# Attention's division by the row sums, moved from the probabilities to o, and two moves beside it

## The chip, the cores and the metric

One NeuronCore of one Trainium2 chip runs the whole block. The time is device microseconds of one execution; the kernel before takes 2336.07 us (median of 3 runs, 2334.95 to 2337.75). The engines are called TensorE (PE), VectorE (DVE), ScalarE (ACT) and GpSimd (POOL); SP's queue issues most of the DMAs, GpSimd's queue the rest.

## The reference, cut to what matters

A layer of 1024 tokens of width 1024: a SwiGLU feed-forward, a mixer, a second SwiGLU feed-forward, each followed by a residual and a layer norm, all in float32. The mixer holds 8 attention heads of 64 columns beside a gated linear recurrence, and an output projection over both. The attention, in blocks of 128 queries:

```python
s = einsum('bhqd,bhkd->bhqk', qh[:, :, q0:q1], kh[:, :, :q1]) * scale
s = s + cum[:, :, q0:q1, None] - cum[:, :, None, :q1]
s = where(mask, s, -1e30)
p = softmax(s, axis=-1)
outs.append(einsum('bhqk,bhkd->bqhd', p, vh[:, :, :q1]))
```

The softmax divides every row of exponentials by its sum. The same o comes out when the values are summed with the exponentials themselves and each row of o is divided by its sum afterwards.

## The kernel before, in words

The stages run one after the other: the first feed-forward (gate/up by Strassen's seven products of blocks, then down), the mixer's input projections with the recurrence, attention with the output projection, the second feed-forward. Every float32 matrix product is done as three matmuls of the type fp32r, of parts called hi and lo: hi is the rounded copy that ScalarE writes, lo is what is left, which VectorE gets by a subtraction.

Attention (`attention`) goes through 64 units, a head h and a block i of 128 queries. Heads 0 to 5 run one after the other, each from i = 7 (1024 keys) down to i = 0 (128 keys); the units of heads 6 and 7 are interleaved. Three functions make a unit:

- `probs(h, i)`: TensorE makes the scores in a bank pair `s` (lines 991 and 992), of which there are two. GpSimd masks the diagonal block of the row `cum`, which is the head's cumulated forget gate, loaded once a head (line 995). VectorE adds cum to the scores, writes p and finds the row's minimum in one instruction (line 997). ScalarE takes the exponential and its sum (line 998). VectorE inverts the sum (line 999) and GpSimd multiplies p by it (line 1000).
- `to_pT(h, i, p)`, three units later: TensorE transposes p in squares of 128 (line 1011) into banks `a`, of which there are four; ScalarE and VectorE write the hi and lo parts `pt` (lines 1015 and 1016).
- `values(h, qt)`, one unit later still and for every second i: TensorE multiplies v by pt for 256 queries (line 1027). ScalarE and VectorE put o together, 64 rows a head, so that heads 2c and 2c + 1 fill one tile of 128 rows whose columns are the queries (lines 1030 and 1031). After the odd head, ScalarE and VectorE write the hi and lo parts `mix` of these 128 rows (lines 1034 and 1035). For heads 1, 3 and 5 GpSimd's queue stores them to memory (line 1038), and SP's queue loads them again shortly before the output projection; those of head 7 are used where they are.

Between the units stand tiles of the output projection (`down_tile`): 16 of them, over the recurrence's part, fill units of heads 0 to 4; the 16 over the attention's part come behind the values of head 7, each followed, when a row block is done, by the layer norm on VectorE and a store of the rows by GpSimd's queue (line 1163). After them the blocks for the second gate/up are transposed and split (line 248).

`load(h)` brings a head's q, k, cum and v; two heads have room. The tiles `raw`, two in number, take weights on their way in: the four halves of the output projection's, and then the first two loads, each in two halves, of the second gate/up (`first_raws`, line 264, called at the end of the kernel function).

The order of the instructions of every engine and queue is fixed when the program is built: a scheduler walks through what the code records, picks by priority and readiness after its own estimates of durations, and gives room in the tile pools and the waits between engines. An engine then works through its own list in that order, each instruction waiting for what it needs. `tc.issue_after(x)` adds one rule: what is recorded in its block stands behind x on x's engine. The tiles `fgz` (128 x 8 x 8), `wf` (128 x 8 x 8) and `gate_raw` (128 x 2 x 128) belong to the mixer's input stage and are not used by attention before the change.

Of the kernel before, what the change touches and what calls it, by code (L numbers as in the profile page):

```python
# [12 lines left out]
AF = mybir.ActivationFunctionType  # L13
ALU = mybir.AluOpType
# [3 lines left out]
P = 128  # L18
# [7 lines left out]
HEADS = 8  # L26
# [22 lines left out]
def f32(ap):  # L49
    return ap.bitcast(F32)  # L50


class Block:
# [903 lines left out]
    def attention(self, w_out, mixp, ln, normed):  # L957

        nc, v = self.nc, self.nc.vector
# [5 lines left out]
        with self.pool("att_p", 3) as pp, self.pool("att_t", 1) as tp, self.pool("att_pt", 6) as ptp, self.pool("att_qk", 2, side="right") as qkp:  # L965

            def load(h):
                vt = qkp.tile([P, NT, P], F32R, tag="v", name=self.nm("v"))
                cum = qkp.tile([P, T], F32, tag="cum", name=self.nm("cum"))
                q, kh, kl = (qkp.tile([P, T], F32R, tag=t, name=self.nm(t)) for t in ("q", "kh", "kl"))  # L970
                mine = slice(64 * (h % 2), 64 * (h % 2) + 64)
                for j in range(2):
                    rows = slice(64 * j, 64 * j + 64)
                    nc.sync.dma_start(f32(q[rows]), self.q_d[h // 2, j, mine, :])
                    nc.sync.dma_start(f32(kh[rows]), self.k_d[h // 2, 0, mine, :])
                    nc.sync.dma_start(f32(kl[rows]), self.k_d[h // 2, 1, mine, :])
                row = self.cum_d[h:h + 1, :]
                nc.sync.dma_start(cum, bass.AP(tensor=row.tensor, offset=row.offset, ap=[[0, P], [1, T]]))
                nc.sync.dma_start(f32(vt), self.v_d[h].rearrange("(j p) d -> p j d", p=P))
                return q, kh, kl, vt, cum  # L980

            def probs(h, i):

                q, kh, kl, _, cum = heads[h]
                n = (i + 1) * P
                ts = slice(i * P, n)
                s = self.s_tile()
                for bank in range((n + H - 1) // H):
                    c1 = min(max(n - bank * H, 256), H)
                    cols = slice(bank * H, bank * H + c1)  # L990
                    mm(s[:, bank, 0:c1], q[:, ts], kh[:, cols], start=True, stop=False)
                    scores = mm(s[:, bank, 0:c1], q[:, ts], kl[:, cols], start=False, stop=True)
                sf = s.rearrange("p b c -> p (b c)")
                p = pp.tile([P, T], F32, tag="p", name=self.nm("p"))
                nc.gpsimd.affine_select(cum[:, ts], cum[:, ts], pattern=[[-1, P]], compare_op=ALU.is_ge, fill=1e30, base=0, channel_multiplier=1)
                m = self.small.tile([P, 4], F32, tag="m", name=self.nm("m"))
                v.tensor_tensor_reduce(p[:, 0:n], sf[:, 0:n], cum[:, 0:n], 1.0, 3e38, ALU.add, ALU.min, m[:, 1:2])
                nc.scalar.activation(p[:, 0:n], p[:, 0:n], AF.Exp, bias=m[:, 1:2], scale=-1.0, accum_out=m[:, 2:3])
                v.reciprocal(m[:, 3:4], m[:, 2:3])
                nc.gpsimd.tensor_scalar(p[:, 0:n], p[:, 0:n], m[:, 3:4], 1.0, op0=ALU.mult, op1=ALU.mult)  # L1000
                return p, scores

            def to_pT(h, i, p):
                if i % 2:
                    pts[h, i // 2] = [tuple(ptp.tile([P, 4, 256], F32R, tag="pt", name=self.nm("pt")) for _ in range(2))
                                      for _ in range((i + 4) // 4)]
                for g in range((i + 4) // 4):
                    js = range(4 * g, min(4 * g + 4, i + 1))
                    pa = self.a_tile()
                    for j in js:  # L1010
                        nc.tensor.transpose(pa[:, (j % 4) * P:(j % 4 + 1) * P], p[:, j * P:(j + 1) * P], self.ident)  # L1011
                    w = len(js)
                    pav = pa.rearrange("p (j t) -> p j t", j=4)[:, 0:w, :]
                    hi, lo = (x[:, 0:w, (i % 2) * P:(i % 2 + 1) * P] for x in pts[h, i // 2][g])
                    nc.scalar.copy(hi, pav)
                    v.tensor_tensor(lo, pav, f32(hi), ALU.subtract)

            def values(h, qt):
                vt = heads[h][3]
                b = h % 2  # L1020
                rows, rest = slice(64 * b, 64 * b + 64), slice(64 - 64 * b, P - 64 * b)
                pv = self.a_tile()
                last = 2 * qt + 1
                for j in range(last + 1):
                    ps = slice(P, 256) if j == last else slice(0, 256)
                    for l in range(2):
                        mm(pv[:, ps], vt[:, j, :], pts[h, qt][j // 4][l][:, j % 4, ps], start=j == 0 and l == 0, stop=j == last and l == 1)  # L1027
                cols = slice(qt * 256, (qt + 1) * 256)
                t = outs[h // 2]
                nc.scalar.copy(t[rows, cols], pv[rest, 0:256])  # L1030
                v.tensor_tensor(t[rows, cols], t[rows, cols], pv[rows, 0:256], ALU.add)
                if b:
                    hi, lo = (x[:, cols] for x in mixes[h // 2])
                    nc.scalar.copy(hi, t[:, cols])
                    v.tensor_tensor(lo, t[:, cols], f32(hi), ALU.subtract)
                    if qt == 0 and h < HEADS - 1:
                        for l in range(2):
                            nc.gpsimd.dma_start(mix_d[h // 2][l], f32(mixes[h // 2][l]))
# [8 lines left out]
            fill = [(i, d) for i in range(NT) for d in range(2)]  # L1047
            AHEAD = 3
            heads[0] = load(0)

            def out_tile():
# [6 lines left out]
            for n in range(len(units) + AHEAD + 1):  # L1058
                if n < len(units):
                    h, i = units[n]  # L1060
                    if i == 5 and h < 6 or (h, i) == (6, 6):
                        heads[h + 1] = load(h + 1)
                    if i == NT - 1:
                        if h % 2 == 0:
                            outs[h // 2] = tp.tile([P, T], F32, tag="o", name=self.nm("o"))
                        else:
                            mixes[h // 2] = tuple(mixp.tile([P, T], F32R, tag="h", name=self.nm("mix")) for _ in range(2))
                    ps[n], scores = probs(h, i)
                if 0 <= n - AHEAD < len(units):
                    to_pT(*units[n - AHEAD], ps.pop(n - AHEAD))  # L1070
                if 0 <= n - AHEAD - 1 < len(units):
                    h, i = units[n - AHEAD - 1]
                    if i % 2 == 0:
                        values(h, i // 2)
                        if h == HEADS - 1:
                            tiles += [(i + 1, 0), (i + 1, 1), (i, 0), (i, 1)]
                if fill and (n < 2 or n % 8 in (2, 3, 4)):
                    i, d = fill.pop(0)
# [16 lines left out]
def kernel(  # L1095
# [7 lines left out]
    nc = tc.nc  # L1103
    blk = Block(ctx, tc)
# [5 lines left out]
    with blk.pool("xl", side="right") as xl, blk.pool("x1") as x1, blk.pool("gu_t", 4) as tp, blk.pool("x22") as x22, \  # L1110
# [13 lines left out]
        raws, load = blk.first_raws(ffn1_w_gate[0], ffn1_w_up[0])  # L1124
# [53 lines left out]
    with blk.pool("xl") as xl, blk.pool("gu_t", 4) as tp, blk.banks() as bank:  # L1178
        blk.open_blocks(xl, REST)
        raws, load = blk.first_raws(ffn2_w_gate[0], ffn2_w_up[0])  # L1180
        load(0)
        load(1)
        finish = blk.gate_up(ffn2_w_gate[0], ffn2_w_up[0], h_d[1], rows, bank, tp, wsp, raws, js=(3, 2, 1, 0))
    right.close()
    with blk.psum(), blk.pool("dn_ws", 10) as blk.wsp, blk.pool("dn_v", side="right") as vp, blk.pool("dn_w", side="right") as wp:
# [40 lines left out]
```

## Time and profile before

| | |
|---|---|
| median of 3 runs | 2336.07 us |
| the profiled execution's own time | 2336.28 us |
| its span, first to last instruction | 2334.6 us |
| TensorE busy | 2305.4 us, 99% |
| VectorE busy | 1632.3 us, 70% |
| ScalarE busy | 1011.3 us, 43% |
| GpSimd busy | 223.0 us, 10% |

Busy time is the union of an engine's instructions. Matmuls overlap one another in the pipeline and their ends are modelled, so TensorE counts as busy for a moment after it has stopped issuing. A matmul of 512 columns is shown for 0.39 us. The time of a stage is read from the stretch in which it runs: attention lies between about 1176 and 1400 us.

### The profile page before, as it was taken

To read this page: it belongs to the slowest core of one execution; us is meant where nothing else is said; L and a number is where in the kernel's file an instruction comes from. 1 tells how busy PE (TensorE), PEld (TensorE's weight loads), DVE (VectorE), ACT (ScalarE), POOL (GpSimd) and SP (SyncE) were. 2 spreads that over 40 slices of the span, in tenths; PEclk is the share of its full clock that TensorE was granted. 3 is DMA by queue.
4 is the path that set the end of the run, shared out by engine and by line. 5 is a ranking of instruction groups with operands and counts; after the bars stand their busy time and mean duration, and the time that the engine had idled before them with its cause. 6 is when DMAs were issued, how large, how long until landed. Compare 5 with 4: busy or idle time off the path is not lost.

```text
span 2334.6 us, 28297 instructions
## 1 busy us (share of the span) xinstructions
PE 2305.4 (99%) x10721; PEld 1915.5 (82%) x10721; DVE 1632.3 (70%) x2509; ACT 1011.3 (43%) x1587; POOL 223.0 (10%) x364
## 2 busy tenths in 40 slices
PE   9999999999999999999999899999999999999998
PEld 7788888888888888888888787888888888888887
DVE  8766566666567888866667899665656565567886
ACT  6443333434344345454546745433333333344342
POOL 0020000000000000011134510000000000000000
PEclk9999999999999999999999999999999999999999
DMA  4333232323465424132365812332323232564531
GB/s 145 129 94 118 86 118 86 117 86 117 144 244 215 164 109 128 56 110 91 109 190 145 244 55 78 112 110 94 118 86 120 92 125 87 182 246 175 181 144 72
DMA packets 175977, 298.93 MB, mean 128 GB/s; under 512 B 8209, under 2 KB 100689, under 8 KB 175841
## 3 DMA queue, kind: packets, MB, share of 16 engines
q1 hardware_dynamic: 152768, 218.16, 28.5%
q0 software_dynamic: 23072, 78.97, 9.2%
q8 instruction: 84, 1.38, 0.2%
q14 instruction: 53, 0.43, 0.1%
HBM read 214.22 MB, written 82.87 MB: 127 GB/s over the span
## 4 chain that ended last, share of the span: by engine, by line
PE 88%; DVE 5%; issue 3%; DMA 2%; ACT 1%; POOL 1%; SPq 0%; DVEq 0%; POOLq 0%; ACTq 0%
PE x L156 9%; PE x L157 9%; PE x L158 9%; PE b L156 7%; PE b L157 7%; PE b L158 7%; PE s L158 6%; PE s L157 6%; PE s L156 6%; PE a L157 6%; PE a L158 6%; PE a L156 6%; PE a L1027 1%; PE a L1011 1%; DMA raw<-in_ffn_w_gate_dram 1%
## 5 line engine op out<-in xcount | busy, mean ns | idle before, releaser
L283 ACT CAST ws<-t 128x512 fp32r<-128x512 f32 x240 | 149.1, 623 | 394.1 <-PE b L157 266.9
L283 ACT CAST ws<-raw 128x512 fp32r<-128x512 f32 x180 | 112.0, 623 | 258.9 <-PE x L157 256.9
L284 DVE TENSOR_TENSOR ws<-raw,ws 128x512 fp32r<-128x512 f32 x180 | 123.8, 688 | 140.3 <-ACT ws L283 136.8
L284 DVE TENSOR_TENSOR ws<-t,ws 128x512 fp32r<-128x512 f32 x240 | 164.3, 685 | 70.5 <-ACT ws L283 68.6
L156 PE MATMUL b<-As,ws 128*128 128x512 f32 x512 | 199.6, 390 | 0.9 <-ACT As L319 0.5
L157 PE MATMUL a<-ws,ws 128*128 128x512 f32 x512 | 199.7, 390 | 0.2
L156 PE MATMUL a<-ws,ws 128*128 128x512 f32 x512 | 199.3, 390 | 0.4 <-ACT row L523 0.4
L157 PE MATMUL b<-As,ws 128*128 128x512 f32 x512 | 199.6, 390 | 0.0
L156 PE MATMUL x<-As,ws 128*128 128x512 f32 x512 | 199.5, 390 | 0.0
L158 PE MATMUL b<-As,ws 128*128 128x512 f32 x512 | 199.3, 389 | 0.0
L158 PE MATMUL x<-As,ws 128*128 128x512 f32 x512 | 199.2, 389 | 0.0
L158 PE MATMUL a<-ws,ws 128*128 128x512 f32 x512 | 199.2, 389 | 0.0
L157 PE MATMUL x<-As,ws 128*128 128x512 f32 x512 | 199.2, 389 | 0.0
L156 PE MATMUL x<-A,ws 128*128 128x512 f32 x496 | 193.5, 390 | 1.0 <-DVE row L517 0.9
L158 PE MATMUL x<-A,ws 128*128 128x512 f32 x496 | 193.2, 390 | 0.7 <-DVE ws L325 0.7
L157 PE MATMUL x<-A,ws 128*128 128x512 f32 x496 | 193.0, 389 | 0.0
L618 ACT CAST ws<-raw 128x1024 fp32r<-128x1024 f32 x112 | 117.4, 1050 | 158.5 <-PE a L157 87.6
L553 POOL DMA_DIRECT2D h_d<-row x96 | 68.8, 719 | 1148.7 <-DVE row L547 1109.6
L621 DVE TENSOR_TENSOR ws<-raw,ws 128x1024 fp32r<-128x1024 f32 x112 | 136.5, 1220 | 50.2 <-ACT ws L618 49.7
L156 PE MATMUL s<-ws,ws 128*128 128x512 f32 x384 | 149.5, 389 | 0.0
L158 PE MATMUL s<-ws,ws 128*128 128x512 f32 x384 | 149.4, 389 | 0.0
L157 PE MATMUL s<-ws,ws 128*128 128x512 f32 x384 | 149.4, 389 | 0.0
(249 smaller groups left out, 5227.1 us busy)
## 6 DMA issues: line engine op xcount, KB each, us to landing
raw<-h_d SPq DMA_DIRECT2D x56, 1024.0 KB, 5.6
h_d<-row POOLq DMA_DIRECT2D x96, 512.0 KB, 3.7
wd<-in_ffn_w_down_dram SPq DMA_DIRECT2D x32, 1024.0 KB, 7.9
raw<-in_ffn_w_gate_dram SPq DMA_DIRECT2D x30, 1024.0 KB, 5.4
raw<-in_ffn_w_up_dram SPq DMA_DIRECT2D x30, 1024.0 KB, 5.4
h_d<-row POOLq DMA_DIRECT2D x32, 256.0 KB, 2.6
raw<-in_w_in_dram SPq DMA_DIRECT2D x16, 512.0 KB, 5.1
row<-in_x_dram SPq DMA_DIRECT2D x12, 512.0 KB, 8.9
```

The lines of the kernel that those rows point to most:

```text
L156: mm(out, ah, bh, start=first, stop=False, skip_group_check=goes_on)
L157: mm(out, ah, bl, start=False, stop=False, skip_group_check=goes_on)
L158: mm(out, al, bh, start=False, stop=last, skip_group_check=goes_on)
L283: nc.scalar.copy(hi, src)
L284: v.tensor_tensor(lo, src, f32(hi), ALU.subtract)
L553: nc.gpsimd.dma_start(d[:, 2 * n:2 * n + 2], t.rearrange("p (r t) -> p r t", r=2))
L618: cast = nc.scalar.copy(hi, src)
L621: self.mark = v.tensor_tensor(lo, src, f32(hi), ALU.subtract)
L1011: nc.tensor.transpose(pa[:, (j % 4) * P:(j % 4 + 1) * P], p[:, j * P:(j + 1) * P], self.ident)
L1027: mm(pv[:, ps], vt[:, j, :], pts[h, qt][j // 4][l][:, j % 4, ps], start=j == 0 and l == 0, stop=j == last and l == 1)
```

## The change

The reciprocal and the multiplication leave `probs`; p stays as the exponentials. The sums go to `fgz`, one column for each head and block. In `to_pT`, for the odd head of a pair and every even i, VectorE inverts the four sums of two heads and two blocks into `wf` in one instruction, and GpSimd copies them, each 64 times, into `gate_raw`. In `values` of the odd head, TensorE transposes the two halves of `gate_raw` into a bank `a`, which gives the reciprocals in the layout of o, and VectorE multiplies the 128 rows and 256 columns of o by them before the hi and lo parts are made. The lo parts of heads 1, 3 and 5 are made by GpSimd, those of head 7 by VectorE as before. Last, the first four loads of the second gate/up stand behind the load of v of the last head in SP's queue.

```diff
--- before.py
+++ after.py
@@ -976,8 +976,10 @@
                     nc.sync.dma_start(f32(kl[rows]), self.k_d[h // 2, 1, mine, :])
                 row = self.cum_d[h:h + 1, :]
                 nc.sync.dma_start(cum, bass.AP(tensor=row.tensor, offset=row.offset, ap=[[0, P], [1, T]]))
-                nc.sync.dma_start(f32(vt), self.v_d[h].rearrange("(j p) d -> p j d", p=P))
+                self.last_load = nc.sync.dma_start(f32(vt), self.v_d[h].rearrange("(j p) d -> p j d", p=P))
                 return q, kh, kl, vt, cum
+
+            sums, inv = self.fgz, self.wf.rearrange("p h i -> p (h i)").rearrange("p (h i) -> p h i", h=HEADS)
 
             def probs(h, i):
 
@@ -995,9 +997,7 @@
                 nc.gpsimd.affine_select(cum[:, ts], cum[:, ts], pattern=[[-1, P]], compare_op=ALU.is_ge, fill=1e30, base=0, channel_multiplier=1)
                 m = self.small.tile([P, 4], F32, tag="m", name=self.nm("m"))
                 v.tensor_tensor_reduce(p[:, 0:n], sf[:, 0:n], cum[:, 0:n], 1.0, 3e38, ALU.add, ALU.min, m[:, 1:2])
-                nc.scalar.activation(p[:, 0:n], p[:, 0:n], AF.Exp, bias=m[:, 1:2], scale=-1.0, accum_out=m[:, 2:3])
-                v.reciprocal(m[:, 3:4], m[:, 2:3])
-                nc.gpsimd.tensor_scalar(p[:, 0:n], p[:, 0:n], m[:, 3:4], 1.0, op0=ALU.mult, op1=ALU.mult)
+                nc.scalar.activation(p[:, 0:n], p[:, 0:n], AF.Exp, bias=m[:, 1:2], scale=-1.0, accum_out=sums[:, h, i:i + 1])
                 return p, scores
 
             def to_pT(h, i, p):
@@ -1014,6 +1014,11 @@
                     hi, lo = (x[:, 0:w, (i % 2) * P:(i % 2 + 1) * P] for x in pts[h, i // 2][g])
                     nc.scalar.copy(hi, pav)
                     v.tensor_tensor(lo, pav, f32(hi), ALU.subtract)
+                if i % 2 == 0 and h % 2:
+                    r = inv[:, h - 1:h + 1, i:i + 2]
+                    v.reciprocal(r, sums[:, h - 1:h + 1, i:i + 2])
+                    nc.gpsimd.tensor_copy(self.gate_raw.rearrange("p u (b d) -> p u b d", b=2),
+                                          r.rearrange("p b u -> p u b").unsqueeze(3).to_broadcast([P, 2, 2, 64]))
 
             def values(h, qt):
                 vt = heads[h][3]
@@ -1030,9 +1035,13 @@
                 nc.scalar.copy(t[rows, cols], pv[rest, 0:256])
                 v.tensor_tensor(t[rows, cols], t[rows, cols], pv[rows, 0:256], ALU.add)
                 if b:
+                    pr = self.a_tile()
+                    for u in range(2):
+                        nc.tensor.transpose(pr[:, u * P:(u + 1) * P], self.gate_raw[:, u], self.ident)
+                    v.tensor_tensor(t[:, cols], t[:, cols], pr[:, 0:256], ALU.mult)
                     hi, lo = (x[:, cols] for x in mixes[h // 2])
                     nc.scalar.copy(hi, t[:, cols])
-                    v.tensor_tensor(lo, t[:, cols], f32(hi), ALU.subtract)
+                    (nc.gpsimd if h < HEADS - 1 else v).tensor_tensor(lo, t[:, cols], f32(hi), ALU.subtract)
                     if qt == 0 and h < HEADS - 1:
                         for l in range(2):
                             nc.gpsimd.dma_start(mix_d[h // 2][l], f32(mixes[h // 2][l]))
@@ -1178,8 +1187,9 @@
     with blk.pool("xl") as xl, blk.pool("gu_t", 4) as tp, blk.banks() as bank:
         blk.open_blocks(xl, REST)
         raws, load = blk.first_raws(ffn2_w_gate[0], ffn2_w_up[0])
-        load(0)
-        load(1)
+        with tc.issue_after(blk.last_load.ins):
+            load(0)
+            load(1)
         finish = blk.gate_up(ffn2_w_gate[0], ffn2_w_up[0], h_d[1], rows, bank, tp, wsp, raws, js=(3, 2, 1, 0))
     right.close()
     with blk.psum(), blk.pool("dn_ws", 10) as blk.wsp, blk.pool("dn_v", side="right") as vp, blk.pool("dn_w", side="right") as wp:
```

## Rows read from the trace of the kernel before

**Rows 1.** Stretches: length, busy us by engine (instructions), TensorE clock, DMA share, GB/s.
```profile
1206.00:1228.20 22.20, 21.83 (x139) 19.34 (x137) 16.34 (x44) 13.51 (x32) 8.24 (x16) 1.00 0.51 120
1284.00:1340.00 56.00, 47.29 (x309) 39.28 (x309) 47.89 (x122) 44.10 (x101) 28.65 (x49) 1.00 0.90 254
1340.00:1400.00 60.00, 59.32 (x312) 48.65 (x312) 55.92 (x130) 27.64 (x61) 9.79 (x20) 1.00 0.13 53
1400.00:1450.00 50.00, 47.72 (x238) 38.67 (x237) 49.86 (x84) 28.26 (x49) 1.06 (x2) 1.00 0.19 64
1475.00:1500.00 25.00, 25.00 (x112) 20.68 (x112) 17.83 (x27) 8.51 (x15) 2.71 (x4) 1.00 0.30 104
```

**Rows 2.** Waits, 1275 to 1400 us: us in total, times, longest.
```profile
PE s L991 <- DVE m L997: 4.3, 8, 1.5
...
DVE m L999 <- ACT p L998: 2.1, 6, 0.6
...
PE a L1011 <- POOL p L1000: 1.5, 3, 0.5
...
PE a L1011 <- DVE pt L1016: 1.2, 2, 0.9
...
PE a L1027 <- DVE pt L1016: 0.9, 1, 0.9
...
PE a L1011 <- DVE m L999: 0.6, 1, 0.6
...
PE a L156 <- DVE o L1031: 0.3, 1, 0.3
```

**Rows 3.** Groups of VectorE, 1175 to 1400 us: busy us, mean ns, idle before.
```profile
L1031 DVE TENSOR_TENSOR o<-o,a 64x256 f32<-64x256 f32 x32 | 13.3, 415 | 5.3 <-ACT o L1030 4.4
L999 DVE RECIPROCAL m<-m 128x1 f32<-128x1 f32 x64 | 10.1, 158 | 7.2 <-ACT p L998 6.7
...
L1035 DVE TENSOR_TENSOR mix<-o,mix 128x256 fp32r<-128x256 f32 x16 | 6.7, 419 | 0.7 <-ACT mix L1034 0.5
```

**Rows 4.** Groups of GpSimd, whole span, the multiplication at two widths.
```profile
L1000 POOL TENSOR_SCALAR p<-p,m 128x1024 f32<-128x1024 f32 x8 | 9.0, 1123 | 0.0
...
L1000 POOL TENSOR_SCALAR p<-p,m 128x256 f32<-128x256 f32 x8 | 3.8, 480 | 5.5 <-DVE m L999 5.4
```

**Rows 5.** GpSimd in order of time: start us, us, instruction, xcount [idle before, releaser].
```profile
1302.35 3.20 POOL L1000 TENSOR_SCALAR p<-p,m 128x896 f32<-128x896 f32 x2
...
1309.36 0.29 POOL L995 TENSOR_SCALAR_AFFINE_SELECT cum<-cum 128x128 f32<-128x128 f32 x1 [3.56 <-DMA cum<-cum_d]
...
1338.25 1.05 POOL L185 TENSOR_SCALAR gb<-gb 128x1024 f32<-128x1024 f32 x1 [2.20 <-DMA gb<-in_ln_g_dram]
...
1353.43 0.58 POOL L1163 DMA_DIRECT2D x_d<-row  x1 [6.28 <-DVE m L999]
```

**Rows 6.** TensorE in order of time: eight transposes in a row, and one alone.
```profile
1283.07 1.04 PE L1011 MATMUL a<-ident,p 128*128 128x128 f32 x8
...
1299.70 0.27 PE L1011 MATMUL a<-ident,p 128*128 128x128 f32 x1
```

**Rows 7.** SP's DMA queue in order of time: start us, us to issue.
```profile
1298.21 0.53 SPq L978 DMA_DIRECT2D cum<-cum_d  x1
...
1304.17 0.53 SPq L264 DMA_DIRECT2D raw<-in_ffn_w_gate_dram  x1
...
1323.15 0.57 SPq L264 DMA_DIRECT2D raw<-in_ffn_w_up_dram  x1
...
1331.45 0.42 SPq L95 DMA_DIRECT2D gb<-in_ln_g_dram  x1
```

**Rows 8.** Tile raw, 1270 to 1420 us: ns min/median/max, first and last start.
```profile
L319 ACT CAST ws<-raw x4: 604/618/626, 1381.5 to 1398.1; 128x512 fp32r<-128x512 f32 x4
```

**Rows 9.** Groups of VectorE, line 999: 1284 to 1340, then 1340 to 1400 us.
```profile
L999 DVE RECIPROCAL m<-m 128x1 f32<-128x1 f32 x21 | 3.3, 158 | 1.4 <-ACT p L998 1.2
...
L999 DVE RECIPROCAL m<-m 128x1 f32<-128x1 f32 x8 | 1.2, 151 | 0.5 <-ACT p L998 0.3
```


## The prediction

> **What bounds the kernel now.** I cut the span into stretches first. In the feed-forward stages TensorE is busy 25.00 of 25.00 us and issues 112 matmuls of 512 columns in them, one every 0.223 us [rows 1]; a change pays only where TensorE pauses or is given less to do. Attention, from about 1176 to 1400 us, is not one stretch but three. Up to 1284 us each head takes about 22 us and TensorE is busy 21.83 of 22.20 us: its matmuls are the bound. From 1284 to 1340 us (heads 4 to 6 and the start of 7), where few output-projection tiles are left to fill in, it is busy 47.29 of 56.00 us: 8.7 us of visible idling, with VectorE at 47.89 and the DMA engines at 0.90 of their time. From 1340 to 1450 us TensorE (59.32 of 60, 47.72 of 50) and VectorE (55.92 of 60, 49.86 of 50) are both nearly full [rows 1]. The change acts in all three, so each gets its own term.
>
> The waits say what ends the 8.7 us: 4.3 us for the score banks, which VectorE's minimum on line 997 sets free late, and 1.5 + 1.2 + 0.9 + 0.6 = 4.2 us at the transposes (line 1011) and values (line 1027), on GpSimd's multiplication, on VectorE's reciprocal ahead of it, or on the low part that follows [rows 2].
>
> **What is removed.** The 64 reciprocals of line 999 take 10.1 us of VectorE, 0.158 each [rows 3], and make VectorE wait for the exponential: 2.1 us of its waiting between 1275 and 1400 us [rows 2]. The 64 multiplications on GpSimd stand between exponential and transposes in every unit: 0.48 us for 256 columns, 1.12 for 1024 [rows 4], and more when something is in the way: two at 1302.35 took 3.20 us together, and at 1309.36 GpSimd stood 3.56 us behind the load of the next head's cum row, with a multiplication queued behind it [rows 5]. Neither remains between exponential and transposes.
>
> **What is added, by engine.** TensorE: two transposes of 128 columns for each of 4 odd heads x 4 column blocks, 32. Eight of line 1011 took 1.04 us together and one lasts 0.27, so the next starts after (1.04 - 0.27) / 7 = 0.11 us [rows 6]; 32 x 0.11 = 3.5 us, 0.88 per odd head. VectorE: 16 reciprocals of 128x2x2, of which no row exists: between the 0.158 of one column and the 0.42 of 128x256 [rows 3]; I take 0.16, as four elements are nearest to one. And 16 multiplications of 128x256 out of PSUM, bounded by line 1031 (0.415, half the partitions) and line 1035 (0.419, from SBUF) [rows 3]: 0.42 each. In heads 1, 3 and 5 the low part of o (0.419 x 4) leaves VectorE and pays for that. Net for VectorE, per head of 8 reciprocals (1.26 us): even heads -1.26, heads 1, 3, 5 -1.26 + 0.64 = -0.6, head 7 -1.26 + 0.64 + 1.68 = +1.1. GpSimd: 16 copies and 12 subtractions of 256 columns, no rows of either; from below VectorE's 0.42, from above the 1.12 of a 1024-column multiplication [rows 3, 4]. I take 0.5, near the 0.48 of the same width; 14 us in all against 64 multiplications of 0.48 us and more [rows 4], so GpSimd gets lighter. The subtractions have only the store of o's parts behind them. New waits: VectorE's multiplication waits for the two transposes, and queued behind it are o's hi and lo parts and the next unit's line 997, which frees a score bank; the transposes wait for GpSimd's copy and take one of the four banks a, 16 times. The copies are read by TensorE one unit later, over 2 us in heads 1 to 6, and that is their cover; without it, each costs TensorE up to 1.1 us.
>
> The Trainium skill (TensorE: Matmul & The Clock Gate, Part 4: PE-mode transpose) gives some 275 ns for one transpose in a kernel. The trace's duration for one agrees (0.27 us), but the next starts 0.11 us later [rows 6]. By the page's figure as a price the 32 would cost 8.8 us, 5.3 more than I charge.
>
> **What is moved.** The four first loads of the second gate/up (512 KB each). Three go out from 1304.17 us on in SP's queue, ahead of head 7's loads and 6 us behind the issue of head 6's cum row (1298.21), for which GpSimd waits until 1309.36; the fourth comes after head 7's v, at 1323.15 [rows 5, 7]. Now all four stand behind that v. Their first reader is at 1381.5 us [rows 8], so they are not late; what they are moved in front of can be: the last mix tiles and gb, gb at 1331.45. GpSimd already waits 2.20 us for gb [rows 5, 7]. At the stretch's 254 GB/s [rows 1] 1.5 MB are 5.9 us. I take zero to come of it, because the engines are 0.90 full from 1284 to 1340 us and the same bytes have left the queue earlier; if that cover fails, head 7's masks behind gb's sign change are late by up to 5.9 us.
>
> **The sum**, against the profiled run's own time, 2336.28 us (span 2334.6 and 1.7 around it); the median of the runs shown, 2336.07, is 0.2 lower.
> - Up to 1284 us, TensorE-bound: heads 1 and 3 pay 1.76 us of transposes. Against that, TensorE idles 0.37 us of a head [rows 1]; half of the 1.1 us of three heads may go as VectorE is freed of the reciprocals. +1.2 us (+0.7 to +1.8).
> - 1284 to 1340 us: the 4.2 us of waits on the multiplication's chain go, and perhaps half (2.1) of the 4.3 us on line 997, since VectorE loses 3.3 us of reciprocals here [rows 9], gains 0.64 for head 5's, and loses its waits for the exponential. Each pause also lasts longer than the idle time shown, since a transpose counts as busy for 0.27 us and the next could have started after 0.11 [rows 6]; ten pauses less, 1.6 us. Head 5 pays 0.9. That is -7.0. What is late next is VectorE itself (47.9 us of work, then about 45) and the cum loads, so I take -6.0. Ends: -10.5 (8.7 + 1.6 all gone, with little paid) and +0.9 (only the transposes seen).
> - From 1340 us on, both engines full: VectorE has head 7's 2.3 us more, less the eight reciprocals left by then (1.2) [rows 9]; TensorE has 0.9 us more. The chain from values to the output tile grows by the multiplication (0.42) and a semaphore, while nine of the tile's twelve matmuls (2.0 us) cover it; as it already stops TensorE once for 0.3 us on o [rows 2], I charge the three together 1.5 us (0 to +4).
> Sum +1.2 - 6.0 + 1.5 = -3.3: **2333.0 us**.
>
> **Rivals.**
> 1. *The middle stretch closes entirely.* For it: nearly half of its waits are by rows the multiplication's [rows 2], and the three loads leave the queue in which head 6's cum is late. Against it: VectorE and the DMA engines are already near full there [rows 1]. -9.5 there, +1.0 before, +1.0 behind: 2328.8 us.
> 2. *Hidden anyway.* VectorE's order, not the multiplication, sets the pace of heads 4 to 6 (the 4.3 us on line 997, and VectorE busy 86%); the freed waits come back on line 997. Then -2.0 in the middle, +1.8 and +1.5 elsewhere: 2337.6 us.
> 3. *GpSimd's queue in head 7 (slower).* The copies of the reciprocals go into the queue that also stores the layer-normed rows, and such a store waits for VectorE: 6.28 us at 1353.43 [rows 5]. A copy behind one makes TensorE stop in order at the two transposes, and no tile passes them. One output tile (12 x 0.223 = 2.7 us) covers part; each costs 3.6 us. Two of them eat up the gain (2333.0 + 7.2 = 2340.2, slower than before); three give 2343.8 us. Against it: multiplications stood in that queue too, and TensorE waits for one three times from 1275 to 1400 us, 1.5 us in all [rows 2].
> 4. *Transposes at their full duration.* If each held TensorE for the 0.27 us that it is shown [rows 6], 32 would cost 32 x 0.16 = 5.1 us more: 2338.1 us. The pace of eight in a row speaks plainly against it. The Trainium skill's figure (TensorE: Matmul & The Clock Gate, Part 4) would be this case.
>
> **Chances.** Forecast (2330.5 to 2335.5) 0.42; rival 1 0.33; rival 2 0.13; rival 3 0.10; rival 4 0.02. A measurement of this kernel tells 0.2%, 4.7 us, from no change: below 2331.4 is faster, above 2340.7 slower. Faster: rival 1 and a part (0.06) of the forecast, 0.39. Slower: rival 3 (0.10) and a late gb with little gain, 0.12. Within: 0.49. The range of 8 in 10 takes rival 1's lower end and rivals 2 and 4, and leaves out most of rival 3: 2326.5 to 2340.0.
>
> **What would show it.** Lines 999 and 1000 are gone, TensorE no longer waits for GpSimd at line 1011, and the stretch from head 4's end to the first output tile of the last heads is 50 us in place of 56, with TensorE over 90% busy. Heads 1 and 3 are each about 0.6 us longer. The four loads stand behind head 7's v and land before 1381 us. TensorE's waits on o and mix after 1340 us sum to no more than 2 us. I am wrong in the cause if the middle keeps its length though those waits are gone (rival 2), and wrong in the sign if TensorE waits at the new transposes for GpSimd (rival 3).

## The result, and the profile after

The changed kernel takes 2347.72 us (median of 4 runs, 2346.22 to 2349.02) where the kernel before takes 2335.51: the quotient of these medians is 1.0052, and the ratio on record, which is used from here on, 1.0043 (95% interval 1.0026 to 1.0061). Measured once more, in other rounds (e8 below), it was 1.0035 (1.0022 to 1.0047). The forecast was 2333.0 us, in a range of 2326.5 to 2340.0; the change is slower, by 8 to 12 us. The profiled execution took 2346.22 us, span 2344.5.

The stretches of the changed kernel, which answer to [rows 1]; columns as there:

```profile
1284.00:1340.00 56.00, 50.13 (x334) 42.49 (x333) 48.49 (x112) 45.82 (x105) 16.76 (x40) 1.00 0.82 234
1340.00:1400.00 60.00, 55.39 (x287) 45.38 (x286) 49.64 (x113) 27.01 (x59) 6.96 (x15) 0.94 0.22 78
1400.00:1450.00 50.00, 47.70 (x243) 40.15 (x242) 49.46 (x89) 24.57 (x47) 1.60 (x3) 0.97 0.14 49
```

From 1284 to 1340 us TensorE is busier (50.13 us for 47.29), as was wanted. Part of that is only that the changed kernel runs 4.5 us late by then and has more of the full stretch in this window: from head 4's first unit to unit (7,5), head 7's block 5, which is the same work in both, TensorE idles 6.1 of 58.8 us where it idled 8.7 of 61.2. From 1340 to 1400 us it lost 3.9 us of work (55.39 for 59.32), and the granted clock, 1.00 before, is 0.94. The waits from 1275 to 1400 us, which answer to [rows 2]:

```profile
POOL gb L185 <- DMA gb<-in_ln_g_dram: 6.3, 1, 6.3
DVE p L999 <- POOL cum L997: 5.3, 4, 4.0
...
PE a L156 <- ACT mix L1043: 4.3, 3, 3.9
PE s L993 <- DVE m L999: 3.2, 6, 1.1
...
PE a L1011 <- DVE o L1036: 0.9, 1, 0.9
...
PE a L1011 <- DVE pt L1016: 0.7, 2, 0.5
PE a L1011 <- ACT p L1000: 0.7, 1, 0.7
```

No wait of TensorE for GpSimd is left at the transposes. In its place stands one long chain, and its links are seen in order of time on SP's queue, GpSimd, VectorE and TensorE. (Line numbers of the changed kernel: the minimum is line 999, the mask 997, the multiplication of o 1041, mix's parts 1043 and 1044, the loads of mix 1095.) SP's queue:

```profile
1326.86 0.38 SPq L979 DMA_DIRECT2D v<-v_d  x1
1327.33 0.53 SPq L264 DMA_DIRECT2D raw<-in_ffn_w_gate_dram  x1
1327.96 0.46 SPq L264 DMA_DIRECT2D raw<-in_ffn_w_up_dram  x1
1328.47 0.77 SPq L264 DMA_DIRECT2D raw<-in_ffn_w_gate_dram  x1
1336.83 1.39 SPq L1095 DMA_DIRECT2D mix<-mix_d  x2
1338.27 1.54 SPq L95 DMA_DIRECT2D gb<-in_ln_g_dram  x1
```

GpSimd, with gb's sign change on line 185 and unit (7,4)'s mask right behind it:

```profile
1337.73 0.29 POOL L997 TENSOR_SCALAR_AFFINE_SELECT cum<-cum 128x128 f32<-128x128 f32 x1 [1.23 <-DVE m L999]
1337.97 0.40 POOL L1020 COPY gate_raw<-wfr 128x256 f32<-128x256 f32 x1
1344.65 1.04 POOL L185 TENSOR_SCALAR gb<-gb 128x1024 f32<-128x1024 f32 x1 [6.28 <-DMA gb<-in_ln_g_dram]
1345.66 0.28 POOL L997 TENSOR_SCALAR_AFFINE_SELECT cum<-cum 128x128 f32<-128x128 f32 x1
```

VectorE at unit (7,4), and TensorE in its first output tile:

```profile
1345.97 0.82 DVE L999 CUSTOM_DVE_ANT_0 p<-s,cum 128x640 f32<-128x640 f32 x1 [4.04 <-POOL cum L997]
```

```profile
1345.44 0.39 PE L158 MATMUL a<-w,mix 128*128 128x512 f32 x1
1349.68 0.79 PE L156 MATMUL a<-w,mix 128*128 128x512 f32 x1 [3.86 <-ACT mix L1043]
1350.28 0.63 PE L157 MATMUL a<-w,mix 128*128 128x512 f32 x1
1350.70 0.63 PE L158 MATMUL a<-w,mix 128*128 128x512 f32 x1
```

gb's load stands in SP's queue behind the load of mix, which waits for GpSimd's store of mix. GpSimd stands 6.28 us for gb, VectorE 4.04 us for the mask behind it; behind that minimum in VectorE's order come o's sum and the multiplication, so the first tile misses the parts of head 7, and TensorE stands 3.86 us. After that its matmuls start 0.42 us apart (1350.28 to 1350.70) where the kernel before has 0.23: for a part of the stretch it ran at the lower of its two levels, 1.2 GHz for 2.4. The kernel before has the same order on GpSimd, with one multiplication between the two, and there it cost next to nothing: gb came at 1338.25 us [rows 5], and VectorE's wait for the same mask was a quarter of a microsecond:

```profile
1340.14 0.82 DVE L997 CUSTOM_DVE_ANT_0 p<-s,cum 128x640 f32<-128x640 f32 x1 [0.26 <-POOL cum L995]
```

### The profile page after: what moved, and what is told of

Read it like the earlier page. It is cut to its first block, busy times and chain, and to the rows that moved or that the text cites. A ratio compares the mean times of both kernels' runs of the same rounds, so it can differ in the third digit from the quotient of the medians.

```text
span 2344.5 us, 28266 instructions
## 1 busy us (share of the span) xinstructions
PE 2310.7 (99%) x10753; PEld 1922.7 (82%) x10753; DVE 1631.1 (70%) x2465; ACT 1011.8 (43%) x1587; POOL 187.0 (8%) x328
## 4 chain that ended last, share of the span: by engine, by line
PE 90%; DVE 4%; issue 3%; ACT 1%; DMA 1%; POOL 0%; SPq 0%; DVEq 0%; POOLq 0%; ACTq 0%
PE x L156 10%; PE x L158 9%; PE x L157 9%; PE b L156 8%; PE b L157 7%; PE b L158 7%; PE s L158 6%; PE s L157 6%; PE s L156 6%; PE a L156 6%; PE a L157 6%; PE a L158 6%; PE a L1032 1%; PE a L1011 1%; PE b L242 1%
```

## The experiments

The table is what all of them are read by. Each number is the difference to the profiled execution of the kernel before, in us, over a stretch that ends at the start of a minimum on VectorE (or, in the last column, at the last matmul). Before, these stand at 1185.48 (head 0's first unit), 1276.62 (head 4's first), 1337.86 (unit (7,5)) and 1348.75 us (unit (6,0)). "Ratio" is the timed one to the kernel before in the same rounds, with its 95% interval. Every number is rounded by itself. Single executions of a kernel lie some 10 us apart (before: 2333.2 to 2344.3), so a profile shows where time went, and the ratio how much.

| kernel | to head 0 | heads 0-3 | head 4 to (7,5) | (7,5) to (6,0) | to the end | sum | ratio |
|---|---|---|---|---|---|---|---|
| changed | +4.0 | +0.5 | -2.5 | +6.7 | +1.2 | +9.9 | 1.0043 (1.0026-1.0061) |
| e8 changed, again | +0.6 | +1.9 | -2.4 | +7.9 | +1.8 | +9.8 | 1.0035 (1.0022-1.0047) |
| e1 changed, loads not moved | +4.4 | +1.9 | -1.9 | +2.0 | +0.8 | +7.2 | 1.0020 (1.0008-1.0031) |
| e3 changed, loads behind gb | +5.0 | +0.6 | -2.4 | +3.8 | +1.2 | +8.3 | 1.0005 (0.9994-1.0016) |
| e4 division alone | +0.8 | +1.0 | +0.7 | +4.3 | +1.7 | +8.6 | 1.0018 (1.0007-1.0028) |
| e5 changed, gb first | +5.9 | +0.6 | +1.4 | +0.2 | +0.7 | +8.9 | 1.0016 (1.0005-1.0027) |
| e6 division alone, gb first | -0.4 | +1.5 | +2.1 | +0.2 | +2.0 | +5.4 | 1.0006 (0.9993-1.0018) |
| e9 changed, gb behind head 6's v | +2.1 | +2.0 | -1.7 | +0.2 | +1.7 | +4.4 | 0.9989 (0.9979-1.0000) |
| e10 the same, low parts on VectorE | +4.7 | +1.7 | -0.3 | +0.2 | +1.0 | +7.2 | 0.9995 (0.9984-1.0005) |
| e2 before, loads moved | -1.3 | +0.3 | -1.7 | 0.0 | +0.1 | -2.6 | 0.9988 (0.9977-0.9999) |
| e7 before, gb first | -0.9 | -1.2 | -0.6 | 0.0 | +0.1 | -2.6 | 1.0001 (0.9991-1.0011) |
| e11 before, loads moved, gb behind v | -0.4 | +0.3 | -2.1 | 0.0 | -0.2 | -2.4 | 0.9984 (0.9973-0.9995) |

**Which part of the change loses the time: four kernels.** e1 takes the move back:

```diff
-        with tc.issue_after(blk.last_load.ins):
-            load(0)
-            load(1)
+        load(0)
+        load(1)
```

> The changed kernel with the four first loads of the second gate/up issued where the kernel before has them (three in the middle of attention); division and low parts as changed. Theory G (the moved loads delay gb, and with it head 7's masks): GpSimd's wait for gb falls from 6.28 us to about 2, VectorE's 4.04 us wait for a mask and TensorE's 3.86 us wait for mix go, the clock stays at 1.00 from 1340 us on, and the time falls by some 6 us, 2347.7 to about 2341.5. If the loss of 4 us at the start of attention is also tied to the move: about 2337. Rival D (the division or GpSimd's low parts lose the time by themselves): 2346 to 2349, unchanged. Rival N (the prediction's forecast for the rest holds once the loads are back): 2333.

e2 is the kernel before with this move alone.

> The kernel before with only the four loads moved behind head 7's v. Theory G: GpSimd waits about 6 us for gb in place of 2.2, and the time grows by some 6 us, 2335.5 to about 2341.5, less if GpSimd's later position in the slower middle hides a part. Rival D: 2335.5, unchanged; the prediction's step (zero for the move) is this too. For the start of attention, whose instructions are the same in all these kernels: if its 4 us belong to the changed program and not to chance, the first minimum of head 0 ends its wait at 1185.5 us here as before.

e3 puts the loads behind gb (`issue_after(blk.fetched.ins)` for `blk.last_load.ins`).

> The changed kernel with the four loads behind gb's second load in place of behind head 7's v. Theory G: mix and gb load with nothing in front, GpSimd's wait for gb falls below 3 us, the waits for head 7's mask and for mix go, and the time is 5 to 8 us below the changed kernel's 2347.7: about 2341. The loads still land before their first reader. Rival D: 2347.7. If the loads' place has no effect but their bytes beside head 7's do: in between, 2344.

e4 has the division alone: e1, and `v.tensor_tensor(lo, ...)` for all heads.

> The kernel before with the division by the sums on o alone: low parts on VectorE as before, the four loads where they were. Theory G: no late gb, so about 2341.5 (only the start of attention lost) or 2336 (if that loss goes too), and within 1.5 us of the changed kernel without the move. Rival L (GpSimd's low parts, which end later and store o's parts later, are what delays mix and gb): 4 us below the changed kernel without the move. Rival D2 (the division itself loses): 2346 or more.

Without the move (e1) and with the loads behind gb (e3) the loss at (7,5) to (6,0) falls from 6.7 to 2.0 and 3.8 us, though GpSimd still waits 4.0 and 4.2 us for gb, more than either expectation allowed. But theory G, as put, fell with e2: the move by itself costs nothing, it gains (0.9988), although GpSimd waits 4.2 us for gb there; the mask of unit (7,4) stands ahead of the sign change in that kernel's order. And e4, with no move at all, loses 4.3 us there: gb is late in all four kernels with the division so far (its sign change at 1343.6 to 1344.7 us), and the moved loads only lengthen it. Rival L misses (1.0018 for e4, 1.0020 for e1, not 4 us apart); D2 has the sign right, at 2343.6 us for 2346: the division alone loses in one place and gains nothing in the middle. e3 is 1.6 us better than expected. In the middle e2 and e4 differ in how full the DMA engines are. First the kernel before from 1305 to 1315 us, then e2 (the last two columns are the engines' share and GB/s):

```profile
1305.00:1310.00 5.00, 3.86 (x31) 3.35 (x30) 3.14 (x8) 3.82 (x9) 1.33 (x4) 1.00 1.06 242
1310.00:1315.00 5.00, 3.91 (x26) 3.00 (x25) 4.03 (x16) 3.21 (x10) 3.01 (x7) 1.00 1.03 316
```

```profile
1305.00:1310.00 5.00, 3.75 (x29) 3.07 (x27) 2.82 (x7) 3.25 (x9) 1.34 (x3) 1.00 0.50 140
1310.00:1315.00 5.00, 4.04 (x28) 3.29 (x26) 4.42 (x17) 3.89 (x12) 2.61 (x6) 1.00 0.38 102
```

The move makes room in a stretch in which they were full. How e2 gets its 1.7 us from that is not shown: GpSimd's wait for head 6's cum row stays (3.5 us for 3.6), and it is TensorE's wait for score banks that falls, from 4.3 to 2.1 us. Without the move, the kernels with the division wait for head 7's k rows: 1.3 us in e1, 3.1 in e6, which is shown here, and 3.3 in e4 at the same place, where the profile names no releaser (TensorE in order of time):

```profile
1326.26 0.76 PE L993 MATMUL s<-kh,q 128*128 128x512 f32 x1 [3.12 <-DMA kh<-k_d]
```

A lower clock follows that stop: 0.83 of full speed in e4 and 0.66 in e6 from 1325 to 1335 us. e1 is the exception to a simple account. It has no move, and its middle is 1.9 us shorter all the same, so the low parts on GpSimd, which e4 lacks, are worth some 2.6 us there; with the move on top (changed, e8) it is 2.4 or 2.5, so the two gains don't add.

**Is it the mask behind gb? gb first.** e5, e6 and e7 load gb six steps earlier, ahead of the first load of mix:

```diff
+                if n == 46:
+                    self.load_gb(*ln, [self.hp.tile([P, T], F32, tag="h", name=self.nm("gb")) for _ in range(2)])
                 if n in MIXES:
...
-                    if len(mix) == 3:
-                        self.load_gb(...)
```

> The changed kernel with gb's two loads and the sign change on GpSimd issued at step 46 of attention, ahead of the first mix load, in place of behind the last mix load at step 52; nothing else. Theory M (in every kernel with the division, unit (7,4)'s mask stands behind gb's sign change, which ended its wait at 1343.6 to 1344.7 us against 1338.25 before; gb is late because its load stands in SP's queue behind the mix load, and that waits for GpSimd's store): the sign change is done before 1325 us, VectorE's wait for that mask (4.04 us in the changed kernel) goes, TensorE's 3.86 us wait for mix shrinks below 1.5, the clock stays at 1.00 after 1340 us, and the time is 5 to 7 us below the changed kernel's in the same rounds: a ratio to the kernel before of about 1.0018. Rival C (the chain from o over the multiplication to mix sets that wait, mask or no mask): TensorE still waits 3 to 4 us for mix and the time stays at 1.004. Rival Q (gb's early load pushes the cum and q loads of head 7 back): the middle gets 2 to 4 us longer and eats the gain.

> The kernel before with the division on o alone (low parts on VectorE, the four loads where they were) and gb loaded and sign-changed at step 46. Theory M: the mask's wait goes, 4 us below the same kernel with gb late (ratio 1.0018 there): 0.9998 to 1.0003, about 2338 to 2339 us beside a before of 2338.7. Rival C: 1.0018 as there. What is left against the forecast of 0.9986 is then the middle, in which the division alone gained nothing (unit (6,7) to (7,5): 0.7 us longer).

> The kernel before with gb loaded and sign-changed at step 46, nothing else. Theory M: there the mask came just in time (mask 1339.81 us, minimum 1340.14 us, VectorE's longest wait for a mask 1.7 us), so at most 1.7 us are gained: ratio 0.9993 to 1.0. If gb's place is worth 4 us or more here too, the late gb is no loss of the change but one of both kernels, and theory M's account of the difference falls.

> The changed kernel once more, to be compared in the same rounds: a ratio of 1.0043 (1.0026 to 1.0061) as first measured, gb's sign change at about 1344.6 us, TensorE's wait for mix 3.9 us. For the start of attention: if the 4 us lost there (TensorE waits 5.7 us for w, ScalarE up to 4.2 us for the stores of v) belong to the program, they are here again and in the changed kernel with gb first, and not in the two kernels with low parts on VectorE; if they are a race that goes one way or the other in each execution, they come and go without that order.

The mask's part of theory M holds in both kernels with the division: from (7,5) to (6,0) they lose 0.2 us where they lost 4 to 8, so rival C falls. e6's ratio, 1.0006, is a little above the expected 0.9998 to 1.0003. e7's ratio says that gb's place is worth nothing to the kernel before. But rival Q is there as well: the 1 MB of gb, put where the DMA engines are full, comes ahead of head 6's cum row, and in e5 GpSimd waits for that:

```profile
1320.37 0.54 POOL L997 TENSOR_SCALAR_AFFINE_SELECT cum<-cum 128x128 f32<-128x128 f32 x2 [5.86 <-DMA cum<-cum_d]
```

The middle then gets 1.4 us longer where it got 2.5 shorter. e5's ratio is still near the expected one (1.0016 for 1.0018), since what it gains behind (7,5) is lost in the middle in part. e8 is no copy of the first profile: the start costs it 0.6 us and not 4.0, and it ends in the same place (+9.8 for +9.9). Half of the 3.4 us was gone by head 4; of the 1.9 left at (7,5), 0.8 went into its longer wait for gb at unit (7,4), which starts at 1344.8 us there and at 1346.0 in the first.

**gb where there is room.** e9, e10 and e11 put gb's loads behind head 6's v, into the stretch that the move had freed:

```diff
+                if n == 47:
+                    with self.tc.issue_after(self.last_load.ins):
+                        self.load_gb(...)
```

> The changed kernel with gb's loads behind head 6's v in SP's queue (where the four moved loads left room: the DMA engines' share from 1305 to 1315 us was 0.44 with the move alone against 1.04 before) and the sign change in head 6; nothing else. Theory M+T (a late gb holds unit (7,4)'s mask; and from head 5 on the DMA engines are full, so that gb's bytes must go where there is room): neither the cum row of head 6 late (as with gb first) nor a wait for a mask in head 7; from unit (7,5) on the distance to the kernel before stays within 1 us until the last unit, and the time is 6 to 7 us below the changed kernel's 2346.2: 2339 to 2340, ratio 1.0005. Rival C (chain from o to mix): 2346. If the bytes are in the way here too: 2343, as with gb first.

> The same with o's low parts on VectorE: the division on o, the four loads moved, gb behind head 6's v. Theory M+T: TensorE's wait of 3.1 to 3.4 us at 1325 us for head 7's k rows (seen in both kernels that had the division and the four loads in the middle) goes with the move; the stretch from head 4's first minimum to unit (7,5)'s is 58.5 to 59.5 us against 61.3 before and 59.5 with the move alone; time 2336 to 2338, ratio 0.9993 to 0.9999. If the low parts on GpSimd are what frees VectorE in the middle: 1 to 2 us above the kernel with them there. The start of attention is expected without its 4 us loss in this kernel and with it, or half of it, in the one with GpSimd's low parts, by what nine profiles showed.

> The kernel before (multiplication on p) with the four loads moved and gb behind head 6's v. Its masks came just in time, so gb's place is worth 0 to 1 us here: 2334 to 2336 us where the kernel before has 2338.5, ratio 0.9985 to 0.9992. If it beats the division with the same loads, the division itself is worth nothing in this kernel, and what there was to gain came from the place of the loads. Rival (the division pays once the loads are out of the way, as the prediction had it): this kernel is 2 to 4 us slower than the one with the division.

In e9 the sign change comes in the middle of head 6 with nothing to wait for, and all that TensorE waits for from 1338 to 1362 us is 0.2 us (first fence: GpSimd; second: TensorE's waits):

```profile
1315.90 1.05 POOL L185 TENSOR_SCALAR gb<-gb 128x1024 f32<-128x1024 f32 x1
```

```profile
PE a L156 <- DVE o L1036: 0.2, 1, 0.2
```

The granted clock from 1340 to 1360 us is 1.00 of full speed (0.83 in the changed kernel, 0.91 in e3 and e4). The ratio goes from 1.0043 and 1.0035 to 0.9989: with gb out of the way the changed kernel is as fast as the kernel before or a little faster. That settles the tail. e11 answers what the division itself is worth: with the same place for the loads, the kernel that still multiplies p is at 0.9984 (0.9973 to 0.9995). It has the lowest ratio of all, and beside e2 it is the only one whose whole interval lies below 1. Its interval and e9's overlap; their medians, from the same rounds, are 2333.8 and 2337.9 us. The rival in e11's expectation, that the division pays once the loads are out of the way and this kernel is 2 to 4 us slower than e9, has no support. TensorE's waits from 1276 to 1342 us show what took the place of the old ones; first e9 (division), then e11 (multiplication):

```profile
PE s L993 <- DVE m L999: 3.3, 6, 1.1
PE a L1011 <- DVE pt L1016: 1.6, 2, 1.1
PE a L1011 <- DVE o L1036: 0.9, 1, 0.9
PE a L1011 <- ACT p L1000: 0.5, 1, 0.5
```

```profile
PE s L991 <- DVE m L997: 2.6, 7, 0.6
PE a L1011 <- POOL p L1000: 1.7, 4, 0.5
PE a L1011 <- DVE m L999: 1.3, 1, 1.3
PE a L1027 <- DVE pt L1016: 0.9, 1, 0.9
PE s L991 <- DVE m L999: 0.8, 1, 0.8
```

The 3.0 us on the multiplication and its reciprocal (1.7 + 1.3) go, and most of it comes back as waits for VectorE: 6.5 us in all in e9, 7.6 in e11. The 1.1 us between them are about the price of head 5's transposes (0.9 in the prediction): from head 4 to (7,5) TensorE is busy 52.8 us in e9 and 51.7 in e11, and the stretch is no shorter (-1.7 for -2.1). In e10, with the low parts on VectorE, TensorE's wait for head 7's k is gone as expected, but the stretch is 60.9 us and not 58.5 to 59.5. Its waits are no longer than e9's (5.6 us in all); but one of them, 1.6 us for VectorE's minimum, is followed by a granted clock of 0.62 and 0.53 from 1337 to 1341 us, where e9 has 1.00. Whether the low parts or the clock cost e10 the 1.4 us against e9 is open.

**The start of attention.** In thirteen profiles TensorE waits there for the first output-projection weights, which ScalarE casts behind v's last parts, whose buffers wait for GpSimd's stores of v: 0.8 to 1.9 us in six of them, 2.2 to 7.5 in seven, though up to there the instructions are the same. In the seven, a 16 KB transfer of code comes some 5 us later than in the six. e10 was expected without this loss and had it (+4.7). e12 is e9 with TensorE's code shifted:

```diff
-        for _ in range(12):
+        for _ in range(60):
             nc.tensor.transpose(warm[:, 0:P], blk.ident, blk.ident)
```

> The changed kernel with gb behind head 6's v, and 48 more warm-up transposes at the very start of TensorE's program (60 in place of 12), so that everything behind them stands 96 instructions later in its code; no other instruction changes. They cost some 11 us at the start by the 0.235 us of the twelve there, and the time is read without them, from the attention stage alone. In seven profiles with a 16 KB code transfer on the DMA queues at 1172.5 to 1174.5 us, amid the loads of head 0, TensorE waited 2.2 to 7.5 us for the first output-projection weights; in the six with that transfer at 1168.1 to 1169.9 us, 0.8 to 1.9 us. Theory F (the transfer's time decides): the shift moves it some 7 us ahead of the loads, and the wait is below 2 us. Rival R (the division's kernels lose it by something else, or the transfer is only a sign of full DMA queues): the wait is 2 us or more although the transfer is out of the way.

The transfer comes at 1166.4 us, 2.5 us ahead of the first load, and the wait is 1.9 us:

```profile
PE a L156 <- ACT w L148: 1.9, 1, 1.9
```

That is theory F's side, if barely: the six end at 1.9 us and the seven begin at 2.2. The sixty take 8.19 us for 2.82, but those behind them, which waited for rows of x before, now run without a wait, and the profile is 1.6 us behind the kernel before at 490 us and 3.0 at 1070, not 11; from head 4 on it is e9's (-1.7, +0.2). Its ratio, 1.0022 (1.0012 to 1.0032), is 7.7 us above e9's, more than the 3.0 that its profile explains.

## Why the prediction was wrong

**What held.** The prices of what is added did, on VectorE: its new reciprocals take 0.170 us (0.16 forecast) and the multiplications 0.418 (0.42), as its groups show:

```profile
L1041 DVE TENSOR_TENSOR o<-o,a 128x256 f32<-128x256 f32 x16 | 6.7, 418 | 0.7
L1019 DVE RECIPROCAL wfr<-fgz 128x4 f32<-128x4 f32 x16 | 2.7, 170 | 1.5 <-ACT p L1000 1.3
```

GpSimd's copies take 0.40 us, its subtractions 0.74, or 0.80 in the mean (0.5 forecast for both), and TensorE waits for neither. Heads 0 to 3 cost 0.5 to 2.0 us (+1.2). No output tile waits for a copy of the reciprocals behind a store of rows, so rival 3 did not come; nor did rival 4, since two new transposes take 0.40 us together where one is shown for 0.27. The waits on GpSimd at the transposes went. And where gb is out of the way (e5, e6, e9, e10), the stretch from (7,5) to the end costs 0.9 to 2.2 us, as the forecast's third term had it (+1.5).

**What failed, first: the moved loads.** The step was "I take zero to come of it, because the engines are 0.90 full from 1284 to 1340 us and the same bytes have left the queue earlier; if that cover fails, head 7's masks behind gb's sign change are late by up to 5.9 us". The cover failed: gb came 6.4 us later (1344.65 for 1338.25). The place and the size were named, the price was not carried into the sum, and the 1.5 us (0 to +4) for all from 1340 us on became 7.9 to 9.6. Two things were missed. One is the slack, and there was none: behind the sign change of [rows 5] GpSimd does one multiplication and the mask, and VectorE already waited 0.26 us for that mask. Whatever made gb later than VectorE was the path's, one for one, and it needed no move (e4): by the ratios the division with gb late costs about as much (e4, 1.0018) as the move on top of it (1.0020 in e1, 1.0035 to 1.0043 with the move). The other is that gb is tied by SP's order to a store: after GpSimd issues the store of mix, the load of mix goes out 3.2 us later in the kernel before (1326.67 to 1329.84) and 6.6 in the changed kernel (1330.18 to 1336.83), where three loads of 512 KB were issued just ahead. All fourteen profiles agree: 2.9 to 3.0 us with no such load issued in the 7 us ahead of the store, 2.9 to 4.6 with one, 4.7 to 5.3 with two, 6.2 to 6.7 with three. That is 3.5 us of gb's 6.4; another 3.5 come of the store, which itself goes out later, and gb's own load is 0.6 us quicker. The Trainium skill (DMA: Bandwidth & Descriptors, Issuing engines are not separate DMA queues) says that transfers run on the same 16 engines whichever engine starts them; the 3.2 and 6.6 us agree, GpSimd's store of 1 MB landing among SP's loads.

**Second: the lower clock.** The forecast had no term for it. TensorE's stop of 3.9 us (4.6 in e8) is followed by a granted clock of 0.83 from 1340 to 1360 us; stops of 2.3 and 1.8 us (e4, e3) by 0.91; one of 1.6 us by 1.00 in e1, but another of 1.6 us by about half speed in e10, so the length of a stop alone doesn't decide. So the 3.8 us at the mask, from (7,5) to (7,4), grow to 6.7 by (6,0); in e1, with the full clock, 1.5 grow to 2.0.

**Third: the middle.** "-6.0" is -2.5 and -2.4; the move alone gives -1.7 (e2), the division with the low parts on GpSimd -1.9 (e1), the division alone +0.7 (e4). Three terms failed. The forecast let 4.2 us of waits go as the multiplication's, but only 1.5 + 0.6 of them were for the multiplication or the reciprocal; the other 1.2 + 0.9 were for the low part pt, which VectorE still writes [rows 2], and e9 has 1.8 us of such waits.

Next, VectorE did not get lighter as it was to. By the forecast's terms its balance is -5.8 us (four even heads at -1.26, three odd ones at -0.6, head 7 at +1.1); its busy time in the whole execution fell from 1632.3 to 1631.1 us, and in e4, where the low parts stay on it, it rose to 1634.6. The price of what is removed was read too high: a reciprocal is shown for 0.158 us, but mostly the next instruction starts 0.08 us after it, as here in the kernel before:

```profile
1340.89 0.16 DVE L999 RECIPROCAL m<-m 128x1 f32<-128x1 f32 x1
1340.97 0.67 DVE L1016 TENSOR_TENSOR pt<-a,pt 128x512 fp32r<-128x512 f32 x1
```

The forecast took the transposes at the pace at which the next one starts and the reciprocals at their full length, so by this pace some 5 of the 10.1 us (64 x 0.08, an estimate) were never there to be saved.

Last, it read the DMA engines' 0.90 as cover for the moved loads and as rival 1's obstacle, and not as a second bound with no room. Without the move head 7's k comes late (e4, e6), with gb first head 6's cum (e5); with the move and gb behind it TensorE waits for VectorE (e9). That is rival 2's result by another road, and rival 2 stood at 0.13. (The lower end, -10.5, is also more than its own terms: 8.7 + 1.6 is 10.3.)

**Fourth: the start.** The sum has no term for it: +4.0 us in the first profile, 0.6 in the same program's second. It isn't the reason of the loss, since both end 10 us late.

The sum of the first profile by the table: +4.0, +0.5 for +1.2, -2.5 for -6.0, +7.9 for +1.5; +9.9 in place of -3.3.

## What to carry to other kernels

Before a load is moved or a stage is made faster, follow what shares the queue: an instruction that waits for a transfer holds all that stands behind it on its engine, so its slack (here none: VectorE already waited 0.26 us for the mask behind gb) is the first number to read. A wait that goes pays only up to the next resource that is full; a DMA share of 0.90 over 56 us may be such a resource, and loads placed by the room in it (e2, e11) were worth more here than the arithmetic that the change saved. And what an instruction costs its engine is the time to the start of the next one, for the work that is removed as well as for the work that is added.

## What the runs showed of the hardware

A late code transfer went with a late stage. In windows of the DMA view around it, the 16 KB transfer (q8 instruction) lies from 1167 to 1171 us in the kernel before and from 1172 to 1176 in the changed one; first before, then changed:

```profile
q1 hardware_dynamic: 192, 0.66, 67.5%
q0 software_dynamic: 50, 0.20, 15.7%
q8 instruction: 1, 0.02, 2.0%
```

```profile
q1 hardware_dynamic: 238, 0.78, 81.8%
q0 software_dynamic: 74, 0.23, 20.1%
q8 instruction: 1, 0.02, 1.9%
```

The Trainium skill (Runtime: NRT & Kernel Launch, Instruction fetch mechanics) says that code comes in blocks of 16 KiB, 256 instructions, fetched ahead and mostly hidden. The size agrees, and no engine is seen waiting for code here; what went with the late transfer, in seven profiles of seven, is TensorE's longer wait for the first output-projection weights. That the transfer causes it is supported by one shifted kernel (e12) and not proved; why it comes late in some programs stays open. The two profiles of one program (changed, e8) both have it late and are 4.0 and 0.6 us behind at head 0, so its price, if it is one, varies by execution.
